# One distance from the weights' buffers for every working tile, and the rest of the input projection from operands without the row factor

## The chip, the cores and the metric

The kernel runs on one core of one Trainium2 chip. The metric is the device time of one execution in microseconds (us); lower is better. Three runs of the kernel before took 1110.45 to 1112.18 us, median 1111.73. The engines are PE (TensorE, matmuls; PEld is its loading of stationary operands), DVE (VectorE), ACT (ScalarE), POOL (GpSimd) and SP, whose queue issues most transfers.

## The reference

Two layers of a hybrid decoder block on 256 tokens of width 1024 in fp32. Cut to what matters:

```python
def layer(x, mem):                       # DEPTH = 2
    h = rmsnorm(x, norm_mix)
    zin = h @ w_in                       # 1024 -> 6840: all heads, and 4 x 1024 gates
    (cq, ckv, kpe, sg_uv, gq, gk, gv, g_lr, g_og, dq, dk, dv, da, db, dz, gates) = split(zin)
    o_a = mla_branch(cq, ckv, kpe)       # latent attention, 4 heads
    o_b = spatial_gating_branch(sg_uv)   # gMLP, chunks of 128
    o_c = gla_branch(gq, gk, gv, g_lr, g_og)
    o_d = deltanet_branch(dq, dk, dv, da, db, dz)
    x = x + sum_i(sigmoid(gates_i) * (o_i @ w_branch_i)) @ w_out
    x = x + cross_attention(rmsnorm(x, norm_xattn), rmsnorm(mem, norm_mem))
    a = relu(rmsnorm(x, norm_mlp) @ w_up)
    return x + (a * a) @ w_down          # 1024 -> 4096 -> 1024

def rmsnorm(x, g):                       # one factor for each token, one gain for each channel
    return x * rsqrt(mean(x * x) + eps) * g

def deltanet_branch(q, k, v, ...):
    qkv = silu(causal_depthwise_conv(concat(q, k, v), conv_w))   # 4 taps: tokens s-3 .. s
```

A final RMSNorm ends the trunk.

## The kernel before

**Layout.** Channels lie on the 128 partitions, tokens in the free dimension. A working tile is 128 x 2 x 256 floats: two blocks of 128 channels by all 256 tokens, 2048 bytes in each partition. The stream `x` is four such tiles.

**Matmuls in three products.** Every large weight is split in two fp32r parts, and so is every operand that it meets. `half()` (L162) takes 1024 columns of weights out of a 1 MB transfer `wr` (3 buffers, issued from SP's queue): ACT copies them to `wh` (L178), DVE makes `wl` as the difference (L181). `wh` and `wl` have four buffers each, 4096 bytes apart in a partition, in a region of their own. `mm3` (L184 to L187) then issues three matmuls into the same bank: `wh` by the high part of the operand (L185), `wh` by its low part (L186) and `wl` by the high part (L187); in the trace L186 is the one whose moving operand ends in `l`. In `gemm` (L203) and `lead4` the 128 x 128 weights are stationary and 256 tokens move; in `gemm_tok` (L233) a block of tokens is stationary and 512 columns of weights move.

**Working tiles.** Nearly all tiles come from one pool `ap`. 44 places `pc0` to `pc43` are handed out first in, first out by `new` and `rel` (L86 to L98). Besides them stand the tiles `hh0` to `hh3`, `hl0` to `hl3` (normalised operand, high and low part) and eight gate tiles that also hold `xh` and `xl`, the operand without the factor of the token (L349 to L353). A place is as large as the largest tile that is ever put there. The convolution's inputs `zc` have three zero columns ahead of the 256 (L455): 2072 bytes, so a place that once holds a `zc` has 2080 bytes, and everything behind it in memory stands 32 bytes further.

**The stages that the change touches.** In each layer the mixers' part of w_in is computed first: five pairs of column blocks from `xh` and `xl` (`ev_dn`, L448, multiplies a bank by the tokens' factor `rrow` on its way out, on DVE), then `hn`, `hh` and `hl` are made (L478 to L489: 8 products, 4 copies and 4 differences in a layer), then `soft_gates` and `conv`, then `zin_rest` (L734), which computes the other blocks and the tokens-first part from `hh` and `hl` and evacuates by plain copies on ACT (L738, L746). Afterwards the four mixers' small matrices, and the gates' 32 column blocks from `hh` and `hl`, which fill PE between the mixers' dependent steps. Behind that: merge, w_out, cross attention, the MLP, and at the end `final` (L1216).

**What sets the order.** A scheduler lays out each engine's queue ahead of time, by program order and priorities: `urgent` evacuations and the making of `wh` and `wl` are moved ahead, and `later` keeps transfers in program order. Every engine then works through its queue in order. A bank of PSUM for `gemm` is one of three.

Of the kernel before, what the change touches and what calls it, by code (L numbers as in the profile page):

```python
# [9 lines left out]
F32 = mybir.dt.float32  # L10
# [6 lines left out]
P = 128  # L17
# [23 lines left out]

N_PIECE = 44
# [13 lines left out]
def decoder(ctx: ExitStack, tc: tile.TileContext, ws, xn_d, xt_d, mem_d, pos_d, fin_d, par_d, cst_d, msk_d, out_d):  # L56
# [12 lines left out]
    def nm(s):  # L69
        uid[0] += 1  # L70
        return f"{s}_{uid[0]}"
# [47 lines left out]
    rsm = cp.tile([P, 2], F32, name="rsm")  # L119

# [222 lines left out]
    def gain(i):  # L343
        return nrm[:, 8 * i : 8 * i + 8]
# [80 lines left out]
    def layer(l):  # L425
# [22 lines left out]
        def ev_dn(p, parts):  # L448
            if p == 0:
                R.rrow = row_of(stat("rsmix"), name="rrow")  # L450
            if p == 2:
                nc.sync.dma_start(pr[:, 0:PC_BS], par_d[l, :, 0:PC_BS])
            if p < 3:
                z = new(shape=(P, 2, T + 3), name="zc")
                G.memset(z[:, :, 0:3], 0.0)  # L455
                zc.append(z)
                z = z[:, :, 3 : T + 3]
            elif p == 3:
                z = R.misc
            else:  # L460
                z = R.gkv = new(name="gkv")
            for c, ps in parts:
                if p == 0:
                    S.copy(z[:, c], ps)
                    ps = z[:, c]
                V.tensor_tensor(z[:, c], ps, bc2(R.rrow, c.stop - c.start), op=ALU.mult)
# [9 lines left out]


        if l == 0:  # L478
            for d, n in ((hh, "hh"), (hl, "hl")):
                d.extend(ap.tile([P, 2, T], F32R, tag=f"{n}{j}", name=nm(n)) for j in range(4))  # L480
        for j in range(4):
            t = new(name="hn")
            for c in range(2):
                V.scalar_tensor_tensor(
                    t[:, c], xs[j][:, c], gain(4 * l)[:, 2 * j + c : 2 * j + c + 1], R.rrow, op0=ALU.mult, op1=ALU.mult
                )
            S.copy(hh[j], t)
            V.tensor_tensor(hl[j], t, hh[j].bitcast(F32), op=ALU.subtract)  # L488
            rel(t)  # L489
# [36 lines left out]
        def conv():  # L526
            qkv = [None] * 3
            stp = bank((P, 2, 8))
            for p in (1, 0, 2):
                cv, th = new(name="cv"), new(name="th")  # L530
                for c in range(2):
                    o = PC_CONV + 4 * (2 * p + c)
                    S.activation(cv[:, c], zc[p][:, c, 0:T], AF.Copy, scale=col(o))
                    for k in range(1, 4):
                        V.scalar_tensor_tensor(cv[:, c], zc[p][:, c, k : k + T], col(o + k), cv[:, c], op0=ALU.mult, op1=ALU.add)
# [198 lines left out]
        def zin_rest():  # L734
            def ev_rest(p, parts):
                ps = parts[0][1]
                t = new(name=("og", "dz", "cq", "su")[p])
                S.copy(t, ps)  # L738
                setattr(R, ("og", "dz", "cq", "su")[p], t)

            gemm(H, L, 8, 4, ev_rest)
            R.zs = []

            def ev_tok(t, ps):
                z = new(name="zs", shape=(P, 512))
                S.copy(z, ps)  # L746
                R.zs.append(z)

            gemm_tok(H, L, 8, ev_tok)
# [309 lines left out]
        zin_rest()  # L1059
        run = [dn(), others()]  # L1060
# [157 lines left out]
    def final(rs, ah, al):  # L1218
# [14 lines left out]
        sq = new(shape=(P, 512), name="sq")  # L1233
        for nb in range(2):

            @urgent
            def evac(t, ps):
# [3 lines left out]
                V.tensor_tensor(z, z, gf[nb], op=ALU.mult)  # L1241
                if nb == 0:
                    return
                rf = rsqrt1(ss[t][:, 0:1], ss[t][:, 1:2], D * EPS, f"rf{t}")
                S.activation(y[t][0], y[t][0], AF.Copy, scale=rf)
                nc.sync.dma_start(out_d[:, t, 0:512], y[t][0])
                V.tensor_scalar(y[t][1], y[t][1], rf, None, op0=ALU.mult)
                S.dma_start(out_d[:, t, 512:1024], y[t][1])

            gemm_tok(ch(ah), ch(al), 32, evac, 4 if nb else 1)  # L1250
        rel(y, gf, sq)
# [186 lines left out]
```

## Time and profile before

| | us |
|---|---|
| median of three runs | 1111.73 |
| profiled execution | 1111.81 |
| its span | 1110.0 |
| PE busy | 1089.8 (98%) |
| DVE busy | 808.9 (73%) |
| ACT busy | 586.8 (53%) |
| POOL busy | 194.5 (18%) |
| transfers | 185.13 MB, 167 GB/s |

The busy time of an engine is a mean over stages; the windows view gives it for a stretch of time, with the number of instructions and the clock that was granted to PE. A row of the list of waits names the engine that waited, its line, and the instruction that ended the wait. A timeline row is start, length, engine, line, and output from inputs. Matmuls overlap in the records: a matmul of 256 columns is shown as 0.28 us long, and the next starts before it ends. How fast PE goes is therefore read from start to start, or from a count of matmuls over a window.

### The profile page before, as it was taken

The numbers are of one execution on the slowest core, as the hardware profiler recorded it, in microseconds if no ns is written. First come the engines' busy times: TensorE is split into PE (matmuls) and PEld (weight loads), VectorE is DVE, ScalarE is ACT, GpSimd is POOL, SyncE is SP. The second block draws the span as 40 slices with busy tenths as digits, with TensorE's granted clock in tenths as the row PEclk, the third lists the DMA queues.
The fourth block names the chain that finished last, engine by engine and source line by source line (L and its number), as shares of the span: only waits on it lengthen the run. The fifth ranks groups of instructions, "written<-read, shape, count | busy, mean of one in ns | idle before, by whom it ended". The sixth has DMA issues, their size and how long they took to land.

```text
span 1110.0 us, 20715 instructions
## 1 busy us (share of the span) xinstructions
PE 1089.8 (98%) x8494; PEld 1046.4 (94%) x8494; DVE 808.9 (73%) x1411; ACT 586.8 (53%) x883; POOL 194.5 (18%) x176
## 2 busy tenths in 40 slices
PE   8899999999999999999999999999999999999996
PEld 8799999999998999999999899999999899998885
DVE  6999848779865866655679997686796777665454
ACT  6475564654644655544455646554454555555342
POOL 6223006108200200000102420310451011010000
PEclk9899999999999999999999999999999999999998
DMA  9344523454543455545545444244455334554541
GB/s 353 141 156 150 182 84 126 141 191 164 187 151 145 175 185 181 185 189 190 190 181 190 153 152 152 84 171 155 165 188 190 133 136 188 190 209 157 190 185 38
DMA packets 28319, 185.13 MB, mean 167 GB/s; under 512 B 3392, under 2 KB 3648, under 8 KB 6976
## 3 DMA queue, kind: packets, MB, share of 16 engines
q1 hardware_dynamic: 26208, 179.09, 44.3%
q10 hardware_dynamic: 2016, 4.72, 1.3%
q8 instruction: 66, 1.08, 0.4%
q14 instruction: 29, 0.24, 0.1%
HBM read 182.75 MB, written 1.05 MB: 166 GB/s over the span
## 4 chain that ended last, share of the span: by engine, by line
PE 94%; DVE 2%; DMA 1%; ACT 1%; issue 0%; ACTq 0%
PE g L186 28%; PE g L185 28%; PE g L187 28%; PE ps L185 1%; PE ps L186 1%; PE ps L187 1%; DMA mr<-memt 1%; PE ps L662 1%; PE ps L658 1%; PE ps L587 1%; DVE wl L181 1%; ACT wh L178 1%; DMA wr<-ws 0%; PE ps L575 0%; PE ps L967 0%
## 5 line engine op out<-in xcount | busy, mean ns | idle before, releaser
L181 DVE TENSOR_TENSOR wl<-wr,wh 128x1024 fp32r<-128x1024 f32 (+1 forms) x337 | 414.6, 1233 | 202.7 <-ACT wh L178 201.8
L178 ACT ACTIVATE wh<-wr 128x1024 fp32r<-128x1024 f32 (+1 forms) x337 | 355.0, 1057 | 352.1 <-PE g L186 254.4
L186 PE MATMUL g<-hl,wh 128*128 128x256 f32 x1280 | 362.5, 283 | 5.3 <-DVE hl L488 5.3
L187 PE MATMUL g<-hh,wl 128*128 128x256 f32 x1280 | 364.1, 285 | 0.0
L185 PE MATMUL g<-hh,wh 128*128 128x256 f32 x1280 | 362.8, 284 | 0.0
L186 PEld LDWEIGHTS g<-hl,wh 128*128 128x128 f32 x1280 | 242.3, 189 | 5.9 <-DVE hl L488 5.5
L187 PEld LDWEIGHTS g<-hh,wl 128*128 128x128 f32 x1280 | 242.0, 189 | 1.0 <-issue 0.3
L185 PEld LDWEIGHTS g<-hh,wh 128*128 128x128 f32 x1280 | 241.8, 189 | 0.7
L187 PE MATMUL g<-ah,wl 128*128 128x256 f32 x256 | 72.0, 281 | 0.0
L186 PE MATMUL g<-al,wh 128*128 128x256 f32 x256 | 71.9, 281 | 0.0
L185 PE MATMUL g<-ah,wh 128*128 128x256 f32 x256 | 71.8, 281 | 0.0
L325 POOL TENSOR_TENSOR sq<-sq,sq 128x512 f32<-128x512 f32 x14 | 21.1, 1506 | 244.8 <-ACT sq L317 244.6
L1093 POOL TENSOR_TENSOR gt<-gt,gt 128x512 f32<-128x512 f32 x16 | 35.6, 2227 | 92.8 <-DVE gt L1092 91.9
L186 PE MATMUL g<-wl,ah 128*128 128x512 f32 x128 | 50.2, 395 | 0.0
L187 PE MATMUL g<-wh,al 128*128 128x512 f32 x128 | 50.1, 394 | 0.0
L185 PE MATMUL g<-wh,ah 128*128 128x512 f32 x128 | 50.0, 395 | 0.0
L185 PEld LDWEIGHTS g<-ah,wh 128*128 128x128 f32 x256 | 48.2, 188 | 0.0
L187 PEld LDWEIGHTS g<-ah,wl 128*128 128x128 f32 x256 | 48.2, 188 | 0.0
L186 PEld LDWEIGHTS g<-al,wh 128*128 128x128 f32 x256 | 48.2, 188 | 0.0
L185 PE MATMUL g<-xh,wh 128*128 128x256 f32 x144 | 39.8, 282 | 1.5 <-ACT xh L298 1.5
L186 PE MATMUL g<-xl,wh 128*128 128x256 f32 x144 | 40.8, 285 | 0.3 <-DVE xl L307 0.3
L187 PE MATMUL g<-xh,wl 128*128 128x256 f32 x144 | 40.4, 283 | 0.0
(500 smaller groups left out, 2276.2 us busy)
## 6 DMA issues: line engine op xcount, KB each, us to landing
wr<-ws SPq DMA_DIRECT2D x166, 1024.0 KB, 4.8
wr<-ws ACTq DMA_DIRECT2D x4, 512.0 KB, 7.7
mr<-memt ACTq DMA_DIRECT2D x8, 256.0 KB, 4.0
par<-par SPq DMA_DIRECT2D x2, 778.0 KB, 6.9
x<-xt SPq DMA_DIRECT2D x3, 256.0 KB, 7.7
cst<-cst SPq DMA_DIRECT2D x1, 588.0 KB, 8.4
gf<-fin SPq DMA_DIRECT2D x2, 256.0 KB, 5.2
yt<-y ACTq DMA_DIRECT2D x2, 256.0 KB, 2.5
```

What stands on the lines that cost most here:

```text
L178: i = S.activation(wh[:, p], r[:, p], AF.Copy)
L181: V.tensor_tensor(wl[:, p], r[:, p], wh[:, p].bitcast(F32), op=ALU.subtract)
L185: PE.matmul(out, ah, bh, start=start, stop=False)
L186: PE.matmul(out, ah, bl, start=False, stop=False)
L187: PE.matmul(out, al, bh, start=False, stop=stop)
L325: G.tensor_tensor(acc, acc, sq, op=ALU.add)
L587: PE.matmul(kk[o][:, 2 * i + c], kT[r, c, ts], src[r, c, ts], start=True, stop=True)
L658: PE.matmul(xp[:, h], M[:, h], Tm[:, h], start=True, stop=True)
L662: PE.matmul(up[:, h], X[t][:, h], U[:, h], start=True, stop=True)
L1093: G.tensor_tensor(gt[m][0], gt[m][0], gt[m][1], op=ALU.add)
```

## The change

Four things are done.

1. **Places.** `zc` loses its three columns and becomes an ordinary tile; its memsets go. The taps are written the other way round: the last tap on all 256 tokens (ACT), then the three others on the tokens from 1, 2 and 3 on. A tile of 48 floats (192 bytes) is put ahead of the pool, and `hh` and `hl` are laid alternately. Every working tile is then 2048 bytes, and all of them stand at the same distance from the weights' buffers, modulo 256 bytes. Counted in the two built programs, for the matmuls of 256 columns with weights as the stationary operand, by the distance of the moving tile from the weights' tile modulo 256:

| distance, bytes | 128 | 32 | 192 | 0 | 64 | 160 | 96 |
|---|---|---|---|---|---|---|---|
| before, matmuls | 5078 | 944 | 422 | 128 | 64 | 48 | 24 |
| after, matmuls | 0 | 0 | 6708 | 0 | 0 | 0 | 0 |

Before, `hh` and `hl` stand at 128, `xh` and `xl` at 32, and the first pair `mgh`, `mgl` of layer 0's w_out at 192. The numbers of matmuls are the same in both, 671 of 512 columns among them.

2. **`zin_rest` from `xh` and `xl`.** Its evacuations multiply by the tokens' factor instead of copying: `og`, `dz`, `cq` and `su` on DVE by `rrow`, `zs` on ACT by a column of factors.

3. **`hn`, `hh` and `hl`** are made behind `zin_rest`, since only the gates need them now.

4. **At the end** the product of the second half with `gf` gets a tile of its own, `yg`, in place of being written over `z`, which the square on ACT reads.

```diff
--- before.py
+++ after.py
@@ -39,6 +39,8 @@
 PC_B136, PC_WG, PC_ALOG, PC_N = 1312, 1448, 1584, 1588
 
 
+
+PAD = 48
 N_PIECE = 44
 
 N_IDLE = 6
@@ -117,6 +119,8 @@
     cs = cp.tile([P, T], F32, name="cs")
     rowm = cp.tile([P, T], F32, name="rowm")
     rsm = cp.tile([P, 2], F32, name="rsm")
+
+    ap.tile([P, PAD], F32, tag="pad", name="pad")
 
 
     raw0 = [wp.tile([P, 2048], F32, tag="wr", name=nm("wr"), bufs=3) for _ in range(2)]
@@ -447,14 +451,13 @@
 
         def ev_dn(p, parts):
             if p == 0:
-                R.rrow = row_of(stat("rsmix"), name="rrow")
+                R.rs = stat("rsmix")
+                R.rrow = row_of(R.rs, name="rrow")
             if p == 2:
                 nc.sync.dma_start(pr[:, 0:PC_BS], par_d[l, :, 0:PC_BS])
             if p < 3:
-                z = new(shape=(P, 2, T + 3), name="zc")
-                G.memset(z[:, :, 0:3], 0.0)
+                z = new(name="zc")
                 zc.append(z)
-                z = z[:, :, 3 : T + 3]
             elif p == 3:
                 z = R.misc
             else:
@@ -473,20 +476,6 @@
         later(pr[:, PC_BS:PC_N], par_d[l, :, PC_BS:PC_N])
         if l == 0:
             later(cst[:, C_TRI:C_N], cst_d[:, C_TRI:C_N])
-
-
-        if l == 0:
-            for d, n in ((hh, "hh"), (hl, "hl")):
-                d.extend(ap.tile([P, 2, T], F32R, tag=f"{n}{j}", name=nm(n)) for j in range(4))
-        for j in range(4):
-            t = new(name="hn")
-            for c in range(2):
-                V.scalar_tensor_tensor(
-                    t[:, c], xs[j][:, c], gain(4 * l)[:, 2 * j + c : 2 * j + c + 1], R.rrow, op0=ALU.mult, op1=ALU.mult
-                )
-            S.copy(hh[j], t)
-            V.tensor_tensor(hl[j], t, hh[j].bitcast(F32), op=ALU.subtract)
-            rel(t)
 
 
         def soft_gates():
@@ -530,9 +519,10 @@
                 cv, th = new(name="cv"), new(name="th")
                 for c in range(2):
                     o = PC_CONV + 4 * (2 * p + c)
-                    S.activation(cv[:, c], zc[p][:, c, 0:T], AF.Copy, scale=col(o))
-                    for k in range(1, 4):
-                        V.scalar_tensor_tensor(cv[:, c], zc[p][:, c, k : k + T], col(o + k), cv[:, c], op0=ALU.mult, op1=ALU.add)
+                    S.activation(cv[:, c], zc[p][:, c], AF.Copy, scale=col(o + 3))
+                    for k in (2, 1, 0):
+                        d = slice(3 - k, T)
+                        V.scalar_tensor_tensor(cv[:, c, d], zc[p][:, c, 0 : T - 3 + k], col(o + k), cv[:, c, d], op0=ALU.mult, op1=ALU.add)
                 S.activation(th, cv, AF.Tanh, scale=0.5)
                 V.scalar_tensor_tensor(cv, th, 1.0, cv, op0=ALU.add, op1=ALU.mult)
                 rel(th)
@@ -735,18 +725,18 @@
             def ev_rest(p, parts):
                 ps = parts[0][1]
                 t = new(name=("og", "dz", "cq", "su")[p])
-                S.copy(t, ps)
+                V.tensor_tensor(t, ps, bc2(R.rrow), op=ALU.mult)
                 setattr(R, ("og", "dz", "cq", "su")[p], t)
 
-            gemm(H, L, 8, 4, ev_rest)
+            gemm(X, XL, 8, 4, ev_rest)
             R.zs = []
 
             def ev_tok(t, ps):
                 z = new(name="zs", shape=(P, 512))
-                S.copy(z, ps)
+                S.activation(z, ps, AF.Copy, scale=R.rs[:, t : t + 1])
                 R.zs.append(z)
 
-            gemm_tok(H, L, 8, ev_tok)
+            gemm_tok(X, XL, 8, ev_tok)
 
         def head_out(n, o, z, gcol, post, pre, name):
 
@@ -1057,6 +1047,21 @@
         if l == 0:
             rope_table()
         zin_rest()
+
+        if l == 0:
+            for j in range(4):
+                for d, n in ((hh, "hh"), (hl, "hl")):
+                    d.append(ap.tile([P, 2, T], F32R, tag=f"{n}{j}", name=nm(n)))
+        for j in range(4):
+            t = new(name="hn")
+            for c in range(2):
+                V.scalar_tensor_tensor(
+                    t[:, c], xs[j][:, c], gain(4 * l)[:, 2 * j + c : 2 * j + c + 1], R.rrow, op0=ALU.mult, op1=ALU.mult
+                )
+            S.copy(hh[j], t)
+            V.tensor_tensor(hl[j], t, hh[j].bitcast(F32), op=ALU.subtract)
+            rel(t)
+
         run = [dn(), others()]
         while run:
             for gen in list(run):
@@ -1231,6 +1236,7 @@
                 S.copy(y[t][nb], ps)
         ss = [small(2, f"ss{t}") for t in range(2)]
         sq = new(shape=(P, 512), name="sq")
+        yg = [new(shape=(P, 512), name="yg") for _ in range(2)]
         for nb in range(2):
 
             @urgent
@@ -1238,17 +1244,19 @@
                 z = y[t][nb]
                 V.scalar_tensor_tensor(z, ps, rs[:, t : t + 1], z, op0=ALU.mult, op1=ALU.add)
                 S.activation(sq, z, AF.Square, accum_out=ss[t][:, nb : nb + 1])
-                V.tensor_tensor(z, z, gf[nb], op=ALU.mult)
                 if nb == 0:
+                    V.tensor_tensor(z, z, gf[nb], op=ALU.mult)
                     return
+                u = yg[t]
+                V.tensor_tensor(u, z, gf[nb], op=ALU.mult)
                 rf = rsqrt1(ss[t][:, 0:1], ss[t][:, 1:2], D * EPS, f"rf{t}")
                 S.activation(y[t][0], y[t][0], AF.Copy, scale=rf)
                 nc.sync.dma_start(out_d[:, t, 0:512], y[t][0])
-                V.tensor_scalar(y[t][1], y[t][1], rf, None, op0=ALU.mult)
-                S.dma_start(out_d[:, t, 512:1024], y[t][1])
+                V.tensor_scalar(u, u, rf, None, op0=ALU.mult)
+                S.dma_start(out_d[:, t, 512:1024], u)
 
             gemm_tok(ch(ah), ch(al), 32, evac, 4 if nb else 1)
-        rel(y, gf, sq)
+        rel(y, yg, gf, sq)
 
     def first_operands(j):
         operands(j, gain(0), True, share=True)
```

The change moves instructions. First PE's queue in layer 0, behind the convolution's products (small matmuls of the row factors and `soft_gates` have lines of their own; names carry the program's numbers). Before:

```order
L185 MATMUL g_427<-xh_225,wh_458 128x256
L186 MATMUL g_427<-xl_226,wh_458 128x256
L187 MATMUL g_427<-xh_225,wl_459 128x256
L496 MATMUL ps_518<-par_105,misc_106 128x136 x2
L185 MATMUL g_636<-hh_490,wh_639 128x256
L185 MATMUL g_697<-hh_490,wh_700 128x256
L186 MATMUL g_636<-hl_494,wh_639 128x256
L187 MATMUL g_636<-hh_490,wl_640 128x256
L185 MATMUL g_636<-hh_490,wh_639 128x256
```

And now, at the same `soft_gates` matmul (L496, now L485):

```order
L191 MATMUL g_606<-xh_154,wl_610 128x256
L189 MATMUL g_606<-xh_154,wh_609 128x256
L190 MATMUL g_606<-xl_155,wh_609 128x256
L485 MATMUL ps_488<-par_106,misc_107 128x136 x2
L191 MATMUL g_606<-xh_154,wl_610 128x256
L189 MATMUL g_606<-xh_190,wh_609 128x256
L190 MATMUL g_606<-xl_191,wh_609 128x256
L191 MATMUL g_606<-xh_190,wl_610 128x256
```

The products of `zin_rest` follow on `xh` and `xl`, 181 of them behind the L485 and then 48 of 512 columns; the first on `hh` stands behind those. In layer 1 it is the same.

Second, DeltaNet's step `s` in layer 0: `uu` and `s` are evacuated by DVE, and each is an operand of two small matmuls on PE. PE's queue before, around `uu`; 34 large matmuls stand between these two small ones and the two on `s` (L703):

```order
L185 MATMUL g_2303<-hh_493,wh_2334 128x256
L698 MATMUL ps_1495<-uu_1488,kd_1087 128x128 x2
L186 MATMUL g_2303<-hl_497,wh_2334 128x256
L187 MATMUL g_2303<-hh_493,wl_2335 128x256
L185 MATMUL g_2303<-hh_493,wh_2334 128x256
```

PE's queue now, where L698 and L703 have become L688 and L693 and stand next to each other:

```order
L189 MATMUL g_2362<-hh_930,wh_2393 128x256
L190 MATMUL g_2362<-hl_931,wh_2393 128x256
L191 MATMUL g_2362<-hh_930,wl_2394 128x256
L688 MATMUL ps_1493<-uu_1486,kd_1085 128x128 x2
L693 MATMUL ps_1498<-s_267_1496,cv_524 128x128 x2
L189 MATMUL g_2423<-hh_924,wh_2426 128x256
L190 MATMUL g_2423<-hl_925,wh_2426 128x256
```

DVE's queue now, from `uu` to `s` (`dd` are the differences of GLA's running sums; L690 was L700):

```order
L685 TENSOR_TENSOR uu_1486<-ps_1487,bro_957 128x256
L810 TENSOR_TENSOR dd_1475<-cum_1466 128x16x8
L811 TENSOR_TENSOR dd_1475<-cum_1466 128x16x8
L810 TENSOR_TENSOR dd_1476<-cum_1466 128x8x16
L811 TENSOR_TENSOR dd_1476<-cum_1466 128x8x16
L810 TENSOR_TENSOR dd_1476<-cum_1466 128x4x32
L811 TENSOR_TENSOR dd_1476<-cum_1466 128x4x32
L810 TENSOR_TENSOR dd_1477<-cum_1466 128x2x64
L811 TENSOR_TENSOR dd_1477<-cum_1466 128x2x64
L804 COPY dd_1477<-cum_1466 128x128
L805 TENSOR_SCALAR dd_1477<-cum_1466 128x128
L690 TENSOR_TENSOR s_267_1496<-ps_1493,cst 128x256
```

Before, the same rows stood between `uu` and `s` on DVE, with a `wl` and four rows of GLA besides. In layer 1 the two small matmuls still have 33 large ones between them. Between DeltaNet's earlier small matmuls (L575, L587, L606, L615, of layer 0) and gMLP's (L1034) stood 2, 7, 11, 15 and 109 large ones; now they are 15, 4 and 15. SP's queue has the same transfers in the same order; POOL's has six memsets less; DVE's carries the evacuations of `og`, `dz`, `cq` and `su`, which ACT's carried.

## The prediction

> **What bounds the kernel now.** The page comes first: its head, the busy line and the shares of the chain that ended last.
>
> ```profile
> span 1110.0 us, 20715 instructions
> PE 1089.8 (98%) x8494; PEld 1046.4 (94%) x8494; DVE 808.9 (73%) x1411; ACT 586.8 (53%) x883; POOL 194.5 (18%) x176
> PE 94%; DVE 2%; DMA 1%; ACT 1%; issue 0%; ACTq 0%
> ```
>
> PE is busy for 98% of the span and is 94% of the chain. So there are only two ways to a shorter time: PE's few waits, and the time from one matmul to the next. The list of PE's waits gives the first.
>
> ```profile
> PE g L186 <- DVE hl L488: 5.3, 1, 5.3
> PE g L185 <- ACT xh L298: 1.5, 1, 1.5
> PE ps L143 <- POOL zc L455: 1.3, 1, 1.3
> PE ps L880 <- DVE sc L873: 1.3, 2, 0.8
> ```
>
> One wait is larger than all others: 5.3 us, once, for the first `hl` of layer 0. For the second, the windows view: its columns are length, busy us and instructions of PE, PEld, DVE, ACT and POOL, then the granted PE clock, the DMA share and GB/s. The first row starts at the matmul that had waited for `hl`, and the second follows it.
>
> ```profile
> 30.00:60.00 30.00, 24.72 (x190) 24.35 (x189) 28.04 (x54) 16.27 (x27) 3.90 (x5) 0.89 0.29 107
> 44.75:49.50 4.75, 4.75 (x21) 4.72 (x22) 4.72 (x9) 0.00 (x0) 0.65 (x1) 0.50 0.32 102
> 49.50:54.25 4.75, 4.75 (x41) 4.75 (x41) 4.66 (x14) 2.12 (x3) 1.71 (x2) 1.00 0.29 119
> 60.00:90.00 30.00, 30.00 (x210) 27.14 (x210) 27.27 (x57) 22.50 (x42) 10.73 (x12) 1.00 0.58 210
> 90.00:120.00 30.00, 30.00 (x259) 29.55 (x258) 29.34 (x103) 14.53 (x23) 7.53 (x7) 1.00 0.31 109
> 120.00:150.00 30.00, 30.00 (x254) 29.63 (x253) 22.80 (x45) 17.65 (x36) 2.73 (x5) 1.00 0.48 171
> 390.00:450.00 60.00, 60.00 (x508) 60.00 (x507) 39.76 (x43) 34.47 (x43) 0.00 (x0) 1.00 0.50 181
> 560.00:586.00 26.00, 26.00 (x225) 26.00 (x225) 21.90 (x45) 15.75 (x26) 2.43 (x2) 1.00 0.49 172
> 600.00:630.00 30.00, 30.00 (x212) 27.27 (x211) 26.52 (x55) 20.02 (x39) 12.27 (x12) 1.00 0.53 194
> 630.00:660.00 30.00, 30.00 (x257) 29.49 (x257) 29.43 (x97) 14.70 (x25) 8.55 (x7) 1.00 0.32 122
> ```
>
> In 390 to 450, PE does nothing but triples of 256-column matmuls on `hh` and `hl`, which lie at distance 128 from the weights' buffers. A matmul is 0.28 us long, so about 2.4 of the 508 only reach in: 60 us over 505.6 is **118.7 ns** from start to start. In 560 to 586 the moving tiles are `xh` and `xl`, at distance 32: 26 us over 222.6 is **116.8 ns**. DVE, ACT and DMA are about as busy in the one as in the other (DVE 66% and 84%), and the busier stage is the quicker one. So the spacing is not set by how much the others do, and the place of the tile is what differs.
>
> Distance 192, at which all tiles stand after the change, occurs in short stretches only: the first tile pair of w_out in layer 0. In PE's timeline every third matmul is an L185; from one row below to the next are six steps where their times lie 0.7 apart.
>
> ```profile
> 281.84 0.28 PE L185 MATMUL g<-mgh,wh 128*128 128x256 f32 x1
> ...
> 282.55 0.28 PE L185 MATMUL g<-mgh,wh 128*128 128x256 f32 x1
> ...
> 283.23 0.28 PE L185 MATMUL g<-mgh,wh 128*128 128x256 f32 x1
> ...
> 288.16 0.28 PE L185 MATMUL g<-mgh,wh 128*128 128x256 f32 x1
> ...
> 288.84 0.28 PE L185 MATMUL g<-mgh,wh 128*128 128x256 f32 x1
> ```
>
> The six on the pair at 192 (from 282.55, and again from 288.16) take 0.68 us, **113.3 ns** each; the six before them, on tiles at other distances, take 0.71, 118.3 ns each. One such head went the other way:
>
> ```profile
> 273.33 0.28 PE L185 MATMUL g<-mgh,wh 128*128 128x256 f32 x1
> ...
> 274.04 0.28 PE L185 MATMUL g<-mgh,wh 128*128 128x256 f32 x1
> ```
>
> **The change part by part.** The profiled execution took 1111.81 us, which is its span of 1110.0 and 1.8 around it; the median of the runs is 1111.73, so nothing has to be converted.
>
> *Places.* 6708 matmuls have 256 columns and a weight tile as the stationary operand: 5078 at distance 128, 944 at 32, 422 at 192, 264 at others (counted in the built program; the table stands with the change). If all go at 113.3 ns: 5078 x 5.4 = 27.4 us, 944 x 3.5 = 3.3, 264 x 5.0 = 1.3, and for the 422, which now stand in short stretches between slower ones, half of 5.4, 1.1. Together **-33.1**. The low end is that the regular place is worth only what `xh` has, 116.8: (5078 x 1.9) + (264 x 1.5) = -10.0; below it, nothing. I take 113.3, since it is the only price for distance 192, and the stretches that have it lie between others that don't. For the 671 matmuls with 512 columns no row tells distances apart: nothing to the same 4.5% of 0.23 us (-7.0). I take nothing.
>
> By the Trainium skill, SBUF — State Buffer, section Who interferes with whom, PE never waits on anyone for the memory, since its moving operand and its weights have a read port each. By that rule the term of the places would be nothing. The rows at 116.8 and 113.3 beside 118.7 don't agree with it; what follows from it is the third case below.
>
> *The rest of the projection from X.* `xh` and `xl` exist long before, so the first matmuls after the convolution's need no `hl`: **-5.3**. The granted clock goes with it: after that wait PE had 0.50 of its clock for 4.75 us and did 21 matmuls, where the next 4.75 us have 41; 20 x 0.116 us is **-2.3**. `hh` and `hl` are first needed some 180 matmuls and 48 of 512 columns later, which is about 32 us.
>
> *What it puts on DVE.* Four evacuations in each layer leave ACT for DVE:
>
> ```profile
> L466 DVE TENSOR_TENSOR misc<-g,rrow 128x512 f32<-128x512 f32 x2 | 1.4, 679 | 0.0
> L738 ACT COPY og<-g x2: 563/566/569, 55.8 to 595.2; 128x512 f32<-128x512 f32 x2
> L181 DVE TENSOR_TENSOR wl<-wr,wh 128x1024 fp32r<-128x1024 f32 x335 | 413.3, 1236 | 196.1 <-ACT wh L178 195.2
> ```
>
> L466 has the same form (a bank times the row factor): 4 x 0.68 = 2.7 us more on DVE; ACT, which loses 4 x 0.57, has room. DVE has none in this stage. From 30 to 120 us it is busy 28.04 + 27.27 + 29.34 = 84.7 of 90, while PE works 24.72 + 30 + 30 = 84.7. After the change DVE has 87.4 to do there. PE has 84.7 - 2.3 for the clock - 3.0 (659 matmuls, 4.5 ns each) = 79.4. DVE becomes what this stage waits for, through `wl` and the banks, and **8.0** of the gain goes back. Bounds: 2, if DVE puts off what isn't `wl` to the stage behind (it is busy 22.8 of 30 there), and 10.6, if it cannot be fuller than now. In layer 1, from 600 to 660, DVE has 26.52 + 29.43 + 2.7 = 58.7 and PE 60 - 2.3 (469 matmuls) = 57.7: **1.0** back (0 to 3).
>
> *Order.* In layer 0 the matmuls of `s` now follow those of `uu` with nothing between, where 34 matmuls stood. Ahead of `s` on DVE, behind `uu`, stand eight rows of differences, a copy and a TENSOR_SCALAR:
>
> ```profile
> L820 DVE TENSOR_TENSOR dd<-cum 128x128 f32<-128x128 f32 x14 | 4.9, 353 | 1.5 <-ACT cum L791 1.5
> L821 DVE TENSOR_TENSOR dd<-cum 128x128 f32<-128x128 f32 x14 | 3.9, 281 | 0.0
> L815 DVE TENSOR_SCALAR dd<-cum 128x128 f32<-128x128 f32 x2 | 1.2, 621 | 0.0
> L700 DVE TENSOR_TENSOR s<-ps,cst 128x256 f32<-128x256 f32 x2 | 0.8, 412 | 0.0
> 176.95 0.61 PE L703 MATMUL ps<-s,cv 128*128 128x128 f32 x4
> ```
>
> 4 x (0.353 + 0.281) + 0.35 for the copy (as L820) + 0.62 + 0.41 = 3.9 us, less some 0.6 of small matmuls (as L703): 3.3 us in which PE, whose queue is in order, stands with all its big matmuls behind. If PE itself comes to `uu` late by the length of a `wl` (1.2 us), some 2.1 stays. I take **+2.2** (0 to 3.3). The DeltaNet's small matmuls ahead of that (L575, L587, L606, L615) have 15, 4 and 15 big ones between them where they had up to 109; when a `wl` is queued ahead of the row that they wait for, each of the three places costs one 1.24: **+3.7** (0 to 8).
>
> *The tail.* The chain ends through
>
> ```profile
> 1101.43 0.73 ACT sq L1240 x2
> 1102.16 0.02 issue
> 1102.18 0.69 DVE y L1241
> ```
>
> With a tile of its own the product no longer waits for the square, and is done beside it: **-0.7** (0 if DVE takes it between the square and the root all the same).
>
> *At nothing:* the taps on 253 to 255 columns instead of 256 (up to 1% shorter, on DVE); six memsets less on POOL, which is 18% busy; the moved `hn` and `hh` (the same instructions, under 32 us of matmuls; uncovered it would be the 5.3 again); ACT's `zs`, a copy that becomes a copy with a factor. SP's queue issues the same transfers in the same order, and the weights came early enough everywhere: PE's list of waits has no DMA.
>
> The sum: -33.1 - 5.3 - 2.3 - 0.7 = -41.4; back 8.0 + 1.0 + 2.2 + 3.7 = 14.9; net -26.5. From 1111.8 that is **1085 us**. With the give-back at its bounds (2 to 25) the same case reaches from 1072 to 1095.
>
> **The rivals.** *The places are worth part of it.* The head at 273.33 stayed at 0.71, and a six-matmul stretch is no stream. At `xh`'s 116.8 everywhere the stream gives 10.0, wait, clock and tail 8.3; DVE's stage gives back 87.4 - (84.7 - 2.3 - 1.0) = 6.0, layer 1 nothing, the order 5.9. Net -6.4: **1105**. For it: it is the only rate other than 118.7 that a long stretch has. Against it: it is `xh`'s price at distance 32, and no stretch at 192 shows it steadily.
>
> *DVE becomes the bound, and no stream pays for it* (slower). If the spacing doesn't go by place, but by which product stands where, the change is: -8.3 for wait, clock and tail, and +5.0 (87.4 against 82.4) + 2.2 + 3.7 on DVE's side, +2.6: **1114**. The place is PE's queue from 60 to 120 us and at `s`; it decides once the stream gives less than 2.6 us, 0.4 ns a matmul. For it: DVE's 29.34 and 27.27 of 30. Against it: three rates with three places, in stages with the same triple of products. This is what the skill's rule on ports would come to.
>
> **How the numbers follow.** The first case 0.66, part of it 0.19, no stream 0.15. The forecast is the first's. Its own range is 1074 to 1095; the second case (1098 to 1108) is needed for 8 in 10: 1074 to 1107. A measurement of this kernel tells about 0.2% (2.2 us) from no change. The first two cases are faster by more than that; of the third, half (0.08) is slower, 0.05 the same, and 0.02 ends faster, since its 11 us of give-back has bounds of 0 and 19. With a hundredth of the second that comes to no change: faster 0.86, same 0.06, slower 0.08.
>
> **What would show it.** In a stage of only `hh` matmuls, 60 us should hold some 530 instead of 508. The wait for `hl` should be gone from the list, and the clock 1.0 from 30 to 60. New rows should stand there, for DVE: `wl`, and `s` at its matmul, some 12 us together before 180 us. DVE should be near 30 of 30 from about 40 to 120. In the chain's tail the product with `gf` should be gone. The forecast is wrong if the stream at 192 keeps 116 or more (then 1105 or over), or if DVE's new waits come to more than 25 us.

## The result: 12 us faster, less than half of what was forecast

The changed kernel takes **1099.18 us** (median of four runs, 1099.05 to 1099.48) where the kernel before took 1111.12 beside it: a ratio of 0.9892, 95% interval 0.9875 to 0.9909. The forecast was 1085, with a range of 1074 to 1107; the sign and the range held, the size did not: 11.9 us instead of 26.5.

The profiled execution took 1099.05 us, 1097.3 of them span. The page's head, the busy line and the chain:

```profile
span 1097.3 us, 20696 instructions
PE 1072.7 (98%) x8494; PEld 1028.3 (94%) x8494; DVE 812.4 (74%) x1419; ACT 583.7 (53%) x875; POOL 196.2 (18%) x170
PE 80%; DVE 11%; ACT 3%; DMA 3%; issue 1%; POOL 1%; ACTq 0%; DVEq 0%; POOLq 0%
```

PE is still busy for 98%, but of the chain it now has 80%, where it had 94%: DVE has come in with 11%. What PE waits for:

```profile
PE g L191 <- DVE wl L185: 3.5, 4, 1.0
PE ps L693 <- DVE s L690: 1.6, 1, 1.6
PE ps L870 <- DVE sc L863: 1.6, 2, 1.0
PE g L189 <- ACT gt L1082: 1.5, 1, 1.5
```

The 5.3 us for `hl` are gone. In their place stand the two that the forecast named, `wl` and `s`, at 3.5 and 1.6 us. The windows view (length, busy us and instructions of PE, PEld, DVE, ACT and POOL, PE clock, DMA share, GB/s), the first three rows in the stage that had that wait, the last inside the MLP:

```profile
30.00:60.00 30.00, 29.96 (x256) 29.64 (x255) 29.15 (x55) 17.91 (x27) 6.67 (x5) 1.00 0.46 162
60.00:90.00 30.00, 26.20 (x168) 22.96 (x169) 29.44 (x56) 19.11 (x28) 11.62 (x11) 1.00 0.49 182
90.00:120.00 30.00, 30.00 (x268) 29.16 (x267) 29.06 (x101) 17.41 (x37) 8.84 (x9) 1.00 0.32 115
...
380.00:440.00 60.00, 60.00 (x511) 60.00 (x511) 41.17 (x50) 34.37 (x43) 0.00 (x0) 1.00 0.53 187
```

The clock is 1.00 from 30 to 60 us, and PE gets through 256 matmuls there instead of 190. From 60 to 90 it stands idle for 3.8 us, with DVE busy for 29.44 of 30. And the row that carries the verdict is the last: the forecast wanted some 530 matmuls in 60 us of the MLP, and there are 511, **117.8 ns** each. So distance 192 does not mean 113.3 ns.

The start-to-start times of the whole trace show what it means. Of the intervals between two matmuls of 256 columns that follow each other without a pause (6,342 of them), the mean is 116.28 ns, where it was 118.54 before; but hardly any stretch has that mean. Stretches of 20 to 1,450 matmuls settle at 113.3 ns, others at 117.8, and a stretch holds its value until other matmuls or a pause interrupt the stream. Below, the first is called the quick phase and the second the slow one. Some stretches, by the time of their first matmul: 23.5 us, 61 matmuls at 113.5; 38.5 us, 179 at 117.8; 352.2 us, 211 at 113.4; 387.1 us, most of the first MLP with its second matrix, 1,450 at 117.8; 585.8 us, 113 at 113.4; 912.9 us, 727 at 117.8. About two thirds are in the slow phase. The 512-column matmuls became quicker too: 230.12 ns on average, where it was 232.19.

### The profile page after: what moved, and what is told of

Its sections match the earlier page's. It is cut to its first block, busy times and chain, and to the rows that moved or that the text cites. A ratio compares the mean times of both kernels' runs of the same rounds, so it can differ in the third digit from the quotient of the medians.

```text
span 1097.3 us, 20696 instructions
## 1 busy us (share of the span) xinstructions
PE 1072.7 (98%) x8494; PEld 1028.3 (94%) x8494; DVE 812.4 (74%) x1419; ACT 583.7 (53%) x875; POOL 196.2 (18%) x170
## 4 chain that ended last, share of the span: by engine, by line
PE 80%; DVE 11%; ACT 3%; DMA 3%; issue 1%; POOL 1%; ACTq 0%; DVEq 0%; POOLq 0%
PE g L189 24%; PE g L191 24%; PE g L190 24%; DVE wl L185 3%; DMA mr<-memt 2%; DVE qt L846 1%; PE ps L189 1%; ACT wh L182 1%; PE ps L191 1%; PE ps L190 1%; DVE gt L1097 1%; PE ps L652 1%; PE ps L648 1%; DMA wr<-ws 1%; DVE mgl L1105 1%
## 5 line engine op out<-in xcount | busy, mean ns | idle before, releaser
L191 PE MATMUL g<-hh,wl 128*128 128x256 f32 x1152 | 325.4, 283 | 3.5 <-DVE wl L185 3.5
L189 PE MATMUL g<-hh,wh 128*128 128x256 f32 x1152 | 324.1, 282 | 2.1 <-ACT gt L1082 1.5
L190 PE MATMUL g<-hl,wh 128*128 128x256 f32 x1152 | 323.2, 281 | 0.0
L191 PEld LDWEIGHTS g<-hh,wl 128*128 128x128 f32 x1152 | 217.0, 188 | 5.4 <-DVE wl L185 4.3
L189 PE MATMUL g<-xh,wh 128*128 128x256 f32 x272 | 75.2, 281 | 1.2 <-ACT xh L302 1.2
L190 PE MATMUL g<-xl,wh 128*128 128x256 f32 x272 | 75.8, 281 | 0.3 <-DVE xl L311 0.3
L191 PE MATMUL g<-xh,wl 128*128 128x256 f32 x272 | 74.9, 280 | 0.0
L189 PEld LDWEIGHTS g<-xh,wh 128*128 128x128 f32 x272 | 51.0, 189 | 1.6 <-ACT xh L302 1.6
L190 PEld LDWEIGHTS g<-xl,wh 128*128 128x128 f32 x272 | 51.2, 189 | 0.5 <-DVE xl L311 0.5
L191 PEld LDWEIGHTS g<-xh,wl 128*128 128x128 f32 x272 | 50.8, 189 | 0.0
```

Of the source, the lines that this page charges most:

```text
L189: PE.matmul(out, ah, bh, start=start, stop=False)
L190: PE.matmul(out, ah, bl, start=False, stop=False)
L191: PE.matmul(out, al, bh, start=False, stop=stop)
```

## The experiments

### The places alone

```diff
+PAD = 48
+    ap.tile([P, PAD], F32, tag="pad", name="pad")
-                z = new(shape=(P, 2, T + 3), name="zc")
+                z = new(name="zc")
...
(the taps and the alternating hh and hl as in the change; nothing else of it)
```

> The kernel before with the places alone: PAD tile, zc without padding, hh and hl laid alternately; PE's order is that of before, row for row. Theory (the places bring the time down, the order gives some of it back): the stream goes from 118.5 to the 116.3 ns that the changed kernel has on average, 6,700 x 2.2 ns = 14.7 us less, the 5.3 us wait for hl stays: 1096 to 1098 us, faster than the whole change. Rival (the gain of the change is the wait for hl, the clock and the tail, and the places add little): 1107 or more.

1097.84 us (1095.73 to 1098.69), ratio 0.9882 (0.9867 to 0.9896). As expected: the places alone bring 13.4 us, as much as the whole change or a little more. The stream's mean is 116.13 ns in the profiled execution, the quickest of the four (span 1093.9), 6,325 x 2.41 = 15.2 us less than before, whose span was 16.1 longer. PE still waits for `hl`, and for little else:

```profile
PE g L189 <- DVE hl L490: 5.6, 1, 5.6
PE ps L883 <- DVE sc L876: 1.9, 2, 1.0
```

### The change without the places

```diff
-    ap.tile([P, PAD], F32, tag="pad", name="pad")
-                z = new(name="zc")
+                z = new(shape=(P, 2, T + 3), name="zc")
...
(the taps and the memsets as before; hh and hl allocated where they were, and made behind zin_rest, which reads xh and xl; yg)
```

> The change without the places: zc padded as before, no PAD tile, hh and hl laid as before (4,500 of the 6,700 matmuls at distance 128, 1,328 at 32), but the rest of the input projection from xh and xl, hn, hh and hl behind it, and yg. Theory: -5.3 for hl, -2.3 for the clock, -0.7 for the tail, and 9 to 12 us given back on DVE's side in 60 to 90 us and at the DeltaNet's steps: 1111 to 1116 us, no faster than before. Rival: the order brings most of the change's 12 us: 1103 or less.

1112.63 us (1111.53 to 1113.94), ratio 1.0015 (1.0005 to 1.0025). The wait, the half clock and the tail are worth 8 us by the rows of before, and all of it is given back. In 60 to 90 us of this kernel:

```profile
30.00:60.00 30.00, 30.00 (x259) 30.00 (x259) 28.29 (x54) 17.73 (x26) 5.85 (x5) 1.00 0.42 147
60.00:90.00 30.00, 26.60 (x168) 23.07 (x167) 29.43 (x54) 19.51 (x29) 9.90 (x9) 1.00 0.50 177
```

PE is never idle from 30 to 60 us, and idle for 3.4 us behind it, at a DVE busy for 29.43 of 30. From 150 to 210 us it is idle for another 3.4, where the kernel before has nothing.

### All tiles at distance 128

```diff
-PAD = 48
+PAD = 32
```

> The changed kernel with one number altered: PAD 32 floats instead of 48, so that every working tile stands at distance 128 instead of 192; the program is otherwise the same, instruction for instruction. Theory (the place sets the matmul's spacing): 118.7 to 120 ns instead of 116.3 on average, 6,700 x 2.4 to 3.7 ns, some of it taken up by PE's waits: 1111 to 1120 us. Rival (PE's two reads of the memory never wait for each other, places do nothing): 1099 us.

1113.94 us (1113.10 to 1114.81), ratio to before 1.0028 (1.0016 to 1.0040). The two programs differ in nothing but addresses, instruction for instruction, and 64 bytes cost 14.8 us. In the same 60 us of the MLP:

```profile
380.00:440.00 60.00, 60.00 (x508) 60.00 (x507) 41.03 (x57) 34.60 (x43) 0.00 (x0) 1.00 0.54 191
```

The stream's mean is 118.96 ns, 2.68 more than at 192; 6,350 of these are 17 us. Some of it is taken up by PE's other waits: PE's idle time (the span less its busy time) is 21.7 us here and 24.6 in the changed kernel.

### A bench of the 16 distances

The model is left out altogether: 96 streams of 48 matmuls with nothing beside them but a small copy. The same triples as in the kernel, at each distance behind each of six kinds of break.

> No part of the model: a bench that leaves the whole computation out. 96 streams of 48 matmuls (the same triples of 256 columns, stationary weights alternating), at the 16 distances 0 to 480 bytes (a to p, in steps of 32), each behind one of six kinds of break: a wait for ACT, none, four 1-column matmuls, two of 128 columns, four of 68, one of 128 in fp32r. Theory (each place has a slow and a quick phase, and a break chooses which): at 192 (g) streams of 113.3 and streams of 117.8 ns and little between, at 128 (e) 118.7 and 120, at 32 (b) 116.7; the same place is found in both phases behind different breaks. Rival (one speed for each place; what varies in the model's stream comes from the work beside it): one value for each place within 0.5 ns whatever the break.

Spacing in ns, the mean of the last 24 intervals (eight triples) of a stream, from the start times in the trace:

| distance | wait for ACT | no break | four of 1 column | two of 128, fp32 | four of 68 | one of 128, fp32r |
|---|---|---|---|---|---|---|
| 0 | left out | 120.0 | 120.0 | 120.0 | 120.0 | 120.0 |
| 32 | 116.7 | 117.8 | 116.7 | 116.7 | 116.7 | 116.7 |
| 64 | 117.8 | 117.8 | 117.8 | 117.8 | 117.8 | 117.8 |
| 96 | 120.0 | 120.0 | 120.0 | 120.0 | 120.0 | 120.0 |
| 128 | 120.0 | 118.5 | 118.6 | 118.7 | 118.8 | 118.8 |
| 160 | 118.6 | 118.8 | 118.8 | 118.7 | 118.6 | 117.3 |
| **192** | **113.3** | **117.8** | **113.3** | **113.3** | **117.8** | **113.3** |
| 224 | 118.3 | 118.3 | 118.3 | 118.3 | 118.3 | 118.3 |

The stream left out is the first of the bench: its first 25 matmuls stand some 214 ns apart, its last ones 120. 256 to 480 repeat these rows, but for one cell: 288 behind a wait has 117.8, the other value of its row. The rival falls: at 192 the same matmuls on the same bytes take 113.3 or 117.8 according to what came before the stream, with the other engines nearly idle. Two streams at 192 (the g in their names), every third matmul, six steps from a row to the next:

```profile
258.26 0.28 PE L78 MATMUL oneg<-mv,w 128*128 128x256 f32 x1
...
258.94 0.28 PE L78 MATMUL oneg<-mv,w 128*128 128x256 f32 x1
...
259.62 0.28 PE L78 MATMUL oneg<-mv,w 128*128 128x256 f32 x1
```

```profile
161.09 0.28 PE L78 MATMUL flowg<-mv,w 128*128 128x256 f32 x1
...
161.80 0.28 PE L78 MATMUL flowg<-mv,w 128*128 128x256 f32 x1
...
162.50 0.28 PE L78 MATMUL flowg<-mv,w 128*128 128x256 f32 x1
```

0.68 and 0.68 in the first, 0.71 and 0.70 in the second. No other distance in steps of 32 has a phase below 116.7. That each place has two phases, as the theory had it, is not shown: 32, 128, 160 and 192 have two values, and 0, 64, 96 and 224 have one behind every break that was tried.

### What changes the phase

A second bench, at 192: the slow phase is set, and odd matmuls are put between streams of 24.

> A bench without any part of the model, at distance 192 unless said: behind a break that set the slow phase before (four 68-column matmuls), 24 matmuls, then one odd matmul (fp32r of 32 to 224 columns, fp32 of 1 or 64, 256 columns at another distance, two halves), 24 matmuls, the same odd matmul, 24, and again. Theory (the phase is kept by the stream and only something irregular changes it): 117.8 stays until an odd matmul; some kinds lead to 113.3 always, others do nothing. Rival (the phase is lost by itself or set by the work beside it): streams change speed between the breaks. Then two other orders of the three products, distances in steps of 4 bytes around 192, and 512-column streams (weights moving) at eight distances: if these have phases too, some of them lie under 231 ns.

Between the odd matmuls no stream changed its speed on its own once settled, over 56 streams. What an odd matmul did, three times each (S 117.8, F 113.3):

| odd matmul | phase before, then behind each of three |
|---|---|
| none but the row of four that should set S | S in 11 of 14 |
| fp32r, 128 columns | S, F, S, F |
| fp32r, 64 | S, F, S, S |
| fp32r, 32 | S, F, S, S |
| fp32r, 160 | S, F, S, S |
| fp32r, 96 | S, F, S, S |
| fp32r, 192 | F, F, F, F |
| fp32r, 224 | F, F, F, F |
| 256 columns at distance 224 or 160 | S, S, S, S (224) and F, F, F, F (160) |
| 256 columns at distance 0 | S, F, F, F |
| 256 columns at distance 96 | S, S, S, S |
| fp32, 1 column | S, F, F, F |
| fp32, 64 columns | S, F, F, F |
| **one product in two halves of 128** | **S, F, F, F** |

The last is the useful one, since a product of the kernel can be issued in this way: it led to F from S once, and kept F twice. It costs 0.12 us: from the matmul ahead of the halves to the third behind them 0.57 us pass, where four steps at 113.3 are 0.45. Below, a product that is issued so is called a cut; the expectations that count 0.06 us a cut are too low by half. The other two orders of the three products have the same phases (117.8 behind the row of four, 113.3 behind a 128). In steps of 4 bytes from 160 to 220 none but 192 is below 117.2. Streams with 512 columns of weights moving showed one speed for each place behind the two breaks that were tried: 226.7 ns at 0, 228.9 at 192, 233.3 to 234.2 at the other six. The kernels show that this is not all: at 192 they have two. In the changed kernel the 383 matmuls from 1000.5 us run at 228.9, and the 47 matmuls from 322.0 us run at 233.3.

### DVE's four evacuations taken back

```diff
-                V.tensor_tensor(t, ps, bc2(R.rrow), op=ALU.mult)
+                S.copy(t, ps)
```

> The changed kernel with og, dz, cq and su evacuated by a copy on ACT as before; the factor of the token is left out on these four (so they are not the reference's). It takes 2.7 us of DVE's work out of each layer. Theory (what the new order gives back is DVE's time from 60 to 120 us): PE's waits there shrink by 2 to 5 us: 1094 to 1097 us. Rival (the give-back is the order of the DeltaNet's steps alone, or the clock): 1098 to 1099.5.

1100.31 us (1099.01 to 1101.66), ratio to before 0.9910 (0.9894 to 0.9927): a miss for the theory. PE's idle time from 60 to 90 us went from 3.8 to 2.4, but DVE stayed full, and another wait came behind it, for `gt` from ACT (1.5 us in the changed kernel), with the clock at 0.89:

```profile
PE g L189 <- ACT gt L1082: 3.7, 2, 2.8
```

```profile
60.00:90.00 30.00, 27.65 (x194) 24.68 (x192) 29.67 (x71) 20.75 (x36) 12.40 (x11) 1.00 0.52 189
...
150.00:180.00 30.00, 26.47 (x228) 24.94 (x227) 16.30 (x44) 14.55 (x30) 9.62 (x10) 0.89 0.30 105
```

Over the whole execution PE is idle for 22.4 us instead of 24.6. The stream's mean was 116.57 instead of 116.28, 1.8 us by itself. Two stretches account for it: those that start with cross attention's last matmul, 211 in each layer, are quick in the changed kernel and slow here (from 353.1 and from 888.5 us), which is 2 x 211 x 4.4 ns = 1.9 us. Others changed as well, and both MLPs are slow in both. A comparison of two orders therefore carries a draw of some 2 us of phases beside the work, and the 1.4 us that PE gained in 60 to 90 cannot be read from the total.

### The wait taken away with one pair

```diff
-            gemm(H, L, 8, 4, ev_rest)
+            if l == 0:
+                gemm(X, XL, 8, 1, ev_rest)
+            gemm(H, L, 8, 4, ev_rest, first=0 if l else 1)
```

on top of the places alone; in layer 0 `og` is multiplied by `rrow` on DVE.

> The places as in the first experiment and the order of the kernel before, but in layer 0 the first of the four pairs of zin_rest (og) comes from xh and xl with the factor on DVE: 48 matmuls, 5.4 us, ahead of the first that needs hl, for 0.7 us of DVE. Theory: the 5.6 us wait goes, the clock with it (2.3), and 1 us or so comes back on DVE: 1090 to 1093 us. Rival (DVE is what this stage waits for, so a wait taken away at its start comes back in it): 1096 to 1099.

1099.59 us (1098.11 to 1101.68), ratio 0.9905 (0.9890 to 0.9920): the rival's number, and a little more than the kernel that it was made from. What PE waits for:

```profile
PE g L190 <- DVE wl L184: 4.6, 4, 2.0
PE g L188 <- ACT xh L301: 1.7, 1, 1.7
PE g L189 <- DVE hl L490: 1.7, 2, 1.4
```

5.6 us for `hl` became 1.7 for `hl` and 4.6 for `wl`. The stage from 30 to 120 us:

```profile
30.00:60.00 30.00, 26.88 (x227) 26.08 (x227) 29.13 (x55) 16.98 (x27) 6.90 (x5) 1.00 0.40 142
60.00:90.00 30.00, 28.60 (x199) 25.43 (x198) 28.62 (x63) 21.93 (x44) 12.25 (x13) 1.00 0.49 176
90.00:120.00 30.00, 27.96 (x232) 27.15 (x232) 27.92 (x94) 13.28 (x21) 6.58 (x6) 0.94 0.31 108
```

PE is idle for 6.6 us of these 90, with the clock at 0.94 in the last third; with the places alone it was 5.8 us, with the clock at 0.89 in the first. It costs DVE one product, 0.7 us, so this is not the evacuations' price: DVE is busy for 84.7 to 87.7 of these 90 us in every order that was tried, and a PE that does not wait at the start waits a little later. (Here too the stream's mean, 116.41, holds 1.8 us of a poorer draw, which is the difference to the kernel that it was made from.)

### The MLP brought into the quick phase

```diff
-    def mm3(out, ah, al, bh, bl, start, stop):
+    def mm3(out, ah, al, bh, bl, start, stop, cut=False):
+        if cut:
+            for q in range(2):
+                c = slice(128 * q, 128 * q + 128)
+                PE.matmul(out[:, c], ah, bh[:, c], start=start, stop=False)
...
-        gemm(H, L, 8, 16, ev_up, lead=True)
+        gemm(H, L, 8, 16, ev_up, lead=True, cut=[(p, m, 4) for p in range(4) for m in range(2)])
```

on the changed kernel: eight products of each MLP in two halves.

> The changed kernel, and in each layer's first MLP matmul eight products (of the first four pairs) are issued as two matmuls of 128 columns instead of one of 256; the result is the same. In the changed kernel both MLP stretches (some 1,750 and 730 matmuls) run at 117.8 ns from their first matmul to their last. Theory (the stream keeps a phase until something irregular comes, and two halves lead to the quick phase, as in the bench): both stretches at 113.3, 2,400 x 4.44 ns = 10.7 us less, 16 x 0.06 = 0.9 more: 1088 to 1091 us. Rival (what keeps the MLP at 117.8 is its own load: weights, DVE, ACT and transfers at once): 1099 to 1100.

1093.44 us (1092.13 to 1093.47), ratio to before 0.9838 (0.9822 to 0.9855), 5.7 us below the changed kernel: far from the rival, and 2.4 us above the range of the theory. PE's timeline at one of these cuts (L192; each third matmul is an L194), and the two MLP windows:

```profile
378.90 0.28 PE L194 MATMUL g<-hh,wh 128*128 128x256 f32 x1
379.25 0.28 PE L194 MATMUL g<-hh,wh 128*128 128x256 f32 x1
379.61 0.33 PE L192 MATMUL g<-hh,wh 128*128 128x128 f32 x2
380.06 0.28 PE L194 MATMUL g<-hh,wh 128*128 128x256 f32 x1
380.40 0.28 PE L194 MATMUL g<-hh,wh 128*128 128x256 f32 x1
380.74 0.28 PE L194 MATMUL g<-hh,wh 128*128 128x256 f32 x1
```

```profile
380.00:440.00 60.00, 60.00 (x530) 60.00 (x530) 42.20 (x52) 35.62 (x45) 0.00 (x0) 1.00 0.53 191
930.00:990.00 60.00, 60.00 (x532) 60.00 (x531) 41.85 (x46) 35.93 (x45) 3.70 (x2) 1.00 0.56 202
```

0.355 a triple before the cut, 0.340 behind it; 530 and 532 matmuls in 60 us instead of 511. DVE, ACT and the transfers do as much as before and more, so the MLP's own load did not keep it slow. Two cuts before this one, at 374.7 and 375.5 us, decide nothing: behind them come four and five matmuls of 256 columns, too few to settle, then the next cut and, at 376.5 us, four 1-column matmuls, and it is behind these that the stream is slow again.

The traces of the three kernels with cuts (this one and the two below) say more than these windows do. Eighty of their 106 cuts have at least eleven matmuls of 256 columns behind them before anything else comes. Behind all 80 the stream settles at 113.3 ns: 20 of them came upon a slow stream, 52 upon a quick one, and 8 upon a piece too short to tell. Slow stretches begin elsewhere: behind other matmuls, or behind a pause of PE. The shortest such pause in the seven kernels at 192 is one interval of 127 ns instead of 113 (as at 796.9 us in the kernel with the four copies on ACT). Without anything of the kind no stretch changed its speed.

That the total gained less than the 10 us of the MLP has two causes. The 16 cuts cost 16 x 0.12 = 1.9 us, and other stretches drew again. The stretch that starts with cross attention's last matmul, 211 in each layer, was quick in the changed kernel and is slow here; in the same 20 us:

```profile
353.00:373.00 20.00, 20.00 (x179) 20.00 (x178) 16.50 (x20) 12.88 (x20) 5.15 (x4) 1.00 0.44 158
```

```profile
353.00:373.00 20.00, 20.00 (x172) 20.00 (x171) 16.13 (x19) 12.87 (x20) 5.16 (x4) 1.00 0.43 158
```

(the changed kernel above, this one below). Layer 1's w_out and 113 matmuls behind the first MLP went the same way; layer 0's w_out went the other. The mean is 115.09: 6,332 x (116.28 - 115.09) = 7.5 us less, 1.9 more for the cuts, together 5.6, and the spans (1097.3 and 1091.7) are 5.6 apart.

### The best that was found

The places alone, with `yg`, and with cuts: 74 of them over all large matmuls (eight in each MLP), and then the MLPs' eight alone. The two expectations count 82 and 66 where the program has 74 and 58: PE has 8,568 matmuls here and 8,494 in the changed kernel.

> The places alone (the first experiment, order of before), with the product of its own tile at the end, and with one product in two halves at the head of most pairs of column blocks in every large matmul, eight in each MLP, 82 in all. Of its 6,325 matmuls 3,860 ran at 117.8. Theory: most of them go to 113.3: 3,000 to 3,500 x 4.44 = 13 to 15.5 us less, 82 x 0.06 = 4.7 more, 0.7 less at the end: 1086 to 1090 us. Rival (a break of any kind sets the phase anew, so the gain outside the MLP is a draw and the cuts cost): 1091 to 1097.

> The kernel of 82 cuts with the eight cuts in each MLP alone: places, order of before, the product of its own tile at the end. Theory (only a long stretch pays for its cuts; elsewhere the next break draws again): 1097.5 - 0.5 for the end - 10.7 + 0.9 for the cuts: 1086 to 1089 us. Rival (the 66 other cuts earn more than their 3.8 us): 1091 or more.

With 74 cuts 1090.67 us (1090.52 to 1092.21), ratio 0.9820 (0.9806 to 0.9835), mean spacing 114.15; with 16 cuts 1090.20 (1088.58 to 1091.01), ratio 0.9811 (0.9795 to 0.9827), mean 114.79. They cannot be told apart, and both are a little above what was expected (by 0.7 and 1.2 us). At 0.12 us a cut the other 58 cost 7.0 us; by the spacing they earn 6,155 x 0.64 ns = 3.9, so they do not pay for themselves in the profiled executions. Both kernels beat the changed kernel by some 9 us, without the move of `zin_rest`.

## Why the prediction was wrong in size

Term by term, against the spans (1110.0 and 1097.3, 12.7 us apart):

| term | forecast | measured |
|---|---|---|
| spacing of the 256-column matmuls | -33.1 | 6,342 x (118.54 - 116.28) = -14.3 |
| wait for `hl` | -5.3 | -5.3 (not in the list any more) |
| half clock | -2.3 | -2.3 (clock 1.00 from 30 to 60) |
| tail | -0.7 | -0.5 |
| 512-column matmuls | 0 | 672 x (232.19 - 230.12) = -1.4 |
| given back on DVE's side and by the order | +14.9 | what is left: +11.1 |

**The step that failed** is "I take 113.3, since it is the only price for distance 192". It was read from six-matmul stretches, and those had the spacing of the quick phase. In the changed kernel a stream at 192 runs at 113.3 or at 117.8, two thirds of it at 117.8, and the term of -33.1 came out at -14.3. The head at 273.33 us, which the prediction showed as one that "went the other way" at 0.71, fits the slow phase (six steps at 117.8 are 0.707). It was the row to build on: at one and the same place there were two spacings, and so the price of a stream was open between 113.3 and 118. The sign that the prediction set for itself, a stream that keeps 116 or more, came true. The rival that took part of the gain put the spacing at 116.8 and the time at 1105; the true mean was 116.28. It had the size of the spacing nearly right by luck, with a reason that did not hold, since nothing runs at that mean for long. The term for the 512-column matmuls, taken as nothing within bounds of 0 to -7.0, was -1.4.

**What held.** Spacing goes by place: 64 bytes of padding, in a program that is otherwise the same, are 14.8 us. By the Trainium skill, SBUF — State Buffer, section Who interferes with whom, PE never waits on anyone; by that the two programs would take the same time. This case's runs do not agree, 1113.94 against 1099.18, and the measurement decides.

**The tail** was nearly right: the product (`yg`) now runs beside the square instead of behind it. It has not left the chain, as the prediction had it, but the chain no longer goes through the square ahead of it. From the last product's evacuation to the end of the span it was 1110.0 - 1100.58 = 9.4 us, and is 8.9:

```profile
1088.42 0.75 DVE y L1245
1089.17 0.07 DVE rf0y L284
1089.23 0.66 DVE yg L1251
```

**The give-back** was right in its places, right in part in its mechanism, and sized too high, 14.9 for 11.1. PE's idle time shows where it stands. From 60 to 90 us it is 3.8 us, where DVE is full (8.0 was forecast). From 600 to 660 us, in layer 1, it is 1.0 (1.0 was forecast). From 150 to 210 us it is 4.1, where the order was to cost 5.9. In the kernel before, PE is idle for less than 0.1 us in all these windows. From 150 to 180 us DVE is not full; PE waits there and up to 210 for `s`, 1.6 us of the 2.2 forecast, and for ACT's `gt`, 1.5 us, which the forecast did not have:

```profile
150.00:180.00 30.00, 28.39 (x263) 27.06 (x262) 17.91 (x44) 15.92 (x29) 10.46 (x10) 1.00 0.30 106
```

One reason for the smaller size may be that PE became less fast than reckoned and so ran less far into DVE; no run separates that. The give-back still eats up the 8 us of the other terms. The places alone have the whole gain, and the rest of the change is worth about nothing, or costs a little: 1112.63 against 1111.24 without the places, 1099.18 against 1097.84 with them. This was in the working, as 14.9 against 8.3, and was not said outright. That DVE's four evacuations are the cause is not shown: taking them back did not bring the time down, and giving DVE only one product was no better. What is shown is that from 30 to 120 us DVE is all but full in every order that was tried.

**Small slips in the working.** The window that starts at the matmul that had waited for `hl` is the one from 44.75 us, not the first of the list. At layer 0's 4.5 ns, layer 1's 469 matmuls give 2.1 us and not 2.3. The first case's lower end is 1072 in the sum and 1074 in the range. None of them bears on the result.

**What stays open.** Why a break leads to the one phase or the other in the kernel. In the bench the same break gave the same phase for most of its kinds; in the kernel, four 1-column matmuls were followed by the slow phase at 376.8 and 912.9 us and by the quick one at 23.4. The order of PE's matmuls does not settle it: the changed kernel and the one with 16 cuts made from it have the same first 1,437 matmuls, and the 63 behind 23.2 us are quick in the one and slow in the other. No run tried which part of PE's two reads sets the spacing. Nor does any run tell the distance from the weights apart from the moving tile's own place modulo 256: the weights' buffers stood at one place in all of them.

## What to carry to other kernels

Measure a stream from start to start and by stretches before pricing it: a mean over a kernel, or a short stretch, can hide two speeds, and the counterexample among five rows is the one to explain. Put the moving tiles at one distance from the stationary ones and try the distances in a bench of some 600 us; it costs one run and decides more than any reordering did here. Taking a wait off the start of a stage in which another engine is full moves the wait and does not remove it.

## What was not expected of the hardware

A stream of alternating weight loads and 256-column matmuls has phases: at one place it runs at 113.3 or at 117.8 ns a matmul (at 128: 118.5 to 118.8 or 120.0), keeps that over up to 1,450 matmuls, and in these traces changed it only behind other matmuls or a pause. With 512 columns there are two speeds as well, 228.9 and 233.3 at 192. Issuing one product in two halves of 128 columns, at 0.12 us, led to the quick phase at all 20 places where a slow stream came upon a cut and had room to settle behind it; in the two MLPs that turned some 1,440 and 700 matmuls. The pattern of places repeats every 256 bytes; in steps of 4 bytes from 160 to 220, 192 alone has the quick phase.
